# One tile of angles for all rotary tables, both halves of the Gram masks in one step, GpSimd's work given to VectorE, and new hand-over times in a two-layer decoder

## The chip, the cores and the metric

The kernel runs on one core of one Trainium2 chip. The metric is device time of one execution in microseconds (us), lower being better: 1338.36 us before, the median of three runs.

## What is computed

Two decoder layers on 512 tokens of width 1024, in float32. Each layer projects the normalized input once, splits the columns over three mixers, joins their outputs in a projection back, and ends in a SwiGLU feed-forward. The reference, cut:

```python
def layer(x):
    hn = rms_norm(x, g1)
    p = hn @ W_in                                   # columns for three mixers
    yA = rwkv7_mixer(p[..., :RW_IN])                # 4 heads x 64, delta-rule state, group norm, gate
    yB = retention_mixer(p[..., RW_IN:RW_IN+RET_IN], positions)   # 4 heads x 64, rotary q and k, decays
    yC = latent_attention(p[..., RW_IN+RET_IN:], positions)       # 8 heads, 64 + 32 rotary
    x = x + concat(yA, yB, yC) @ W_out
    return x + swiglu(rms_norm(x, g2))
...
def rope(x, positions):
    d = x.shape[-1]
    inv = ROPE_BASE ** (-arange(0, d, 2) / d)
    ang = positions[..., None] * inv
    x1, x2 = x[..., : d // 2], x[..., d // 2:]
    return concat([x1 * cos(ang) - x2 * sin(ang), x2 * cos(ang) + x1 * sin(ang)])
```

## The kernel before

**Tiles.** Activations lie feature-major, in tiles of 128 features by 512 tokens. A float32 product is made of three products of rounded halves: every operand is split in a high part and a low part (high + low = value), and `gemm` issues for each block of 128 input features (a k-step) high x high, low x high and high x low, so three matmuls of 128x512, all at line L244 (`mm`). Weights come by SP's DMA into `wr` (512 KB); ScalarE casts the high part `wh` (L404), VectorE subtracts to get the low part `wl` (L405), or GpSimd does it for the weights whose numbers stand in `POOL_LO`. There are three buffers of each. PSUM has four buffers `pd` (projections, attention scores) and four buffers `pm` (everything else).

**Order.** The stages are Python generators that a `Driver` resumes. Its clock counts modelled TensorE time; `yield T[l]["name"]` says how much of it passes before the generator is resumed, and the entries `p_...` are priorities. TensorE's instructions keep the order in which they are issued so; on the other engines a scheduler sets the order from when things are issued. The table `EN` gives many element-wise operations (`E("e595")` and the like) to VectorE (`d`), GpSimd (`p`) or ScalarE (`a`). So a number in `T` moves instructions on every engine.

**Rotary tables** (`tables`, `angles`, L527 to L583). The positions times a column of frequencies, reduced to [-pi, pi] by eight operations of VectorE, then Abs and two Sin of ScalarE. Done once for retention (`invr`, then a sign by GpSimd at L571, two DMAs to `tab_d`), once for the keys of attention in another layout, and once for its queries (`invm`, two DMAs at L580). L1131/L1132 and L1260/L1261 read the tables back.

**RWKV** (`rwkv`). Low-rank products (operands `LR`) give decay and gates. Sums over heads normalize the key (L656 takes their maximum with 1e-24, then L657, L663). Per block b of 128 channels, ScalarE makes three exponentials (L707 to L709), and four products make the operands of the Gram matrices: e592 (L716), e593 (L717), e594 (L718) on VectorE and e595 (L720) on GpSimd, with a small `dsc` (L721). L726 and L308 make and split the bonus term. Then four Gram groups (two per block) of 16 matmuls 64x128 each fill two `pm` buffers; L744 and L745 mask their parts into `GL` and `GR`, 32 operations of 128x256 per layer. L747 sends `GL` to `ms_d` for the solve of 31 steps (L792, L793). `chain` runs the eight chunks of each block one after the other and copies each output back into the operand `ar` (L862); `group_norm` splits it (casts L870 on ScalarE, subtractions h4 L871 on VectorE), forms mean and variance on TensorE, and ends at L882 to L887.

**Rotary step** (L1140 to L1145). L1140 scales a projection, four DMAs of SP swap its halves, GpSimd multiplies with cosine (e968, L1143) and sine (e969, L1144), VectorE adds (L1145). Attention's queries go through L1265 to L1272 (e1090, e1096, e1097) and L1285 into the score operands; `head` makes scores (TensorE, 96 rows), the maximum (L974), exp on ScalarE (L976), the reciprocal (L978) and the scaling (L979).

**Feed-forward.** Four pairs of gate and up projections are made plainly (L1343 to L1346), the rest in Strassen-Winograd form on 2x2 blocks of 128x512 weights (sums at L433, split at L422 and L423) and of tokens. `token_sums` (L1008 to L1052) makes the eight token operands B11, -T1, B22, -T2, B21, T4, T3, each a high and a low tile of 128x1024 (L1015 to L1029), handing over by `sums1` to `sums7`; TensorE uses them in the order -T1, B11, B22, -T2, a down projection, B21, T4.

Of the kernel before, what the change touches and what calls it, by code (L numbers as in the profile page):

```python
# [41 lines left out]
NU, NR, NW = 29, 8, 3  # L42

AHEAD, FETCH = 3, 2
POOL_LO = (20, 35, 38, 115, 137, 139)


def shape_constants():
# [142 lines left out]
def tile_trunk(ctx: ExitStack, tc: tile.TileContext, a: dict, out: bass.AP, dbg=None):  # L191
# [334 lines left out]
    def tables():  # L526
# [44 lines left out]
        for i, u in enumerate((co, si)):  # L571
            sp.dma_start(tab_d[i], u)
# [906 lines left out]
```

## Time and profile before

| | |
|---|---|
| median of three runs | 1338.36 us (1336.69 to 1338.86) |
| profiled execution | 1338.68 us, span 1336.9 us |
| mean granted clock of TensorE | 0.977 |
| TensorE busy | 1282.5 us (96%) |
| weight loads busy | 1095.1 us (82%) |
| VectorE busy | 993.8 us (74%) |
| ScalarE busy | 690.1 us (52%) |
| GpSimd busy | 123.0 us (9%) |

The span is the time from the first to the last instruction; the profiled execution's own time is 1.8 us more. PE is TensorE, PEld its weight loads, DVE VectorE, ACT ScalarE, POOL GpSimd, SP the engine that issues most DMAs. In a row of the timeline stand the start, the duration, engine, line, operation, what is written and read, the shapes and a count; in brackets is the idle time of the engine just before, with what ended it. The granted clock is 1.00 at full speed.

### The profile page before, as it was taken

Reading aid. Unit: us, or ns where it says so; the run is one execution under the profiler, and the core shown is the slowest. Engines: PE = TensorE matmul, PEld = TensorE weight load, DVE = VectorE, ACT = ScalarE, POOL = GpSimd, SP = SyncE. Lnnn points to the kernel's source line nnn. Section 1 sums busy time; section 2 is a strip of 40 time slices with the busy share of each in tenths; the row PEclk is TensorE's granted clock in tenths of the full one; section 3 lists DMA queues with packets and bytes.
Section 4 is the critical chain, followed back from the end, with each engine's and each line's share of the span. In section 5 each row is a group of like instructions: output and inputs, shape, how many; then the busy total and the mean of one; then the engine's idle time right before and its main releaser. Section 6 shows DMA issues by size and latency. Waiting matters only on the chain. (4 is left out here: it accounts for less than half of the span.)

```text
span 1336.9 us, 20195 instructions
## 1 busy us (share of the span) xinstructions
PE 1282.5 (96%) x7774; PEld 1095.1 (82%) x7774; DVE 993.8 (74%) x1672; ACT 690.1 (52%) x1279; POOL 123.0 (9%) x102
## 2 busy tenths in 40 slices
PE   7989999899899999999999898989999999999996
PEld 5768787578799999999877777846888999999994
DVE  7796877747977777777658696586579877777774
ACT  7844446726444444455475345556355545444553
POOL 0151131201000000000004400121010000000000
PEclk9989999999899999999999899979999999999998
DMA  7434421223142333333522424121222333322231
GB/s 243 129 96 135 93 79 55 79 64 111 35 139 96 100 106 95 100 107 101 183 88 83 126 78 85 33 95 63 79 95 79 111 106 100 110 96 95 82 109 63
DMA packets 65593, 131.04 MB, mean 98 GB/s; under 512 B 29045, under 2 KB 31765, under 8 KB 65497
## 3 DMA queue, kind: packets, MB, share of 16 engines
q1 hardware_dynamic: 64120, 128.14, 31.0%
q8 instruction: 61, 1.00, 0.3%
q10 hardware_dynamic: 1232, 1.09, 0.2%
q0 software_dynamic: 144, 0.52, 0.1%
q14 instruction: 36, 0.29, 0.1%
HBM read 117.40 MB, written 9.18 MB: 95 GB/s over the span
## 5 line engine op out<-in xcount | busy, mean ns | idle before, releaser
L244 PE MATMUL pd<-u,wh 128*128 128x256 f32 (+1 forms) x3112 | 760.8, 337 | 9.8 <-ACT wh L404 6.3
L244 PEld LDWEIGHTS pd<-u,wh 128*128 128x128 f32 x3112 | 531.0, 192 | 74.4 <-issue 7.8
L244 PE MATMUL pd<-u,wl 128*128 128x256 f32 (+1 forms) x1556 | 519.0, 334 | 1.4 <-DVE wl L423 1.4
L244 PEld LDWEIGHTS pd<-u,wl 128*128 128x128 f32 x1556 | 298.7, 192 | 30.6 <-DVE wl L423 1.9
L244 PE MATMUL pm<-u,wh 128*128 128x512 f32 (+1 forms) x800 | 212.1, 352 | 0.1
L404 ACT CAST wh<-wr 128x1024 fp32r<-128x1024 f32 (+3 forms) x102 | 98.8, 974 | 165.2 <-PE pd L244 97.2
L244 PEld LDWEIGHTS pm<-u,wh 128*128 128x128 f32 x800 | 139.1, 190 | 18.5 <-DVE u L1025 0.3
L405 DVE TENSOR_TENSOR wl<-wr,wh 128x1024 fp32r<-128x1024 f32 (+3 forms) x96 | 113.4, 1184 | 43.3 <-ACT wh L404 43.2
L244 PE MATMUL pm<-u,wl 128*128 128x512 f32 (+1 forms) x400 | 140.4, 351 | 0.0
L422 ACT CAST wh<-r 128x512 fp32r<-128x512 f32 x144 | 87.4, 618 | 101.5 <-PE pm L244 52.5
L422 ACT CAST wh<-wr 128x512 fp32r<-128x512 f32 x108 | 67.0, 620 | 78.3 <-PE pm L244 55.6
L423 DVE TENSOR_TENSOR wl<-r,wh 128x512 fp32r<-128x512 f32 x144 | 97.6, 687 | 9.4 <-ACT wh L422 7.5
L423 DVE TENSOR_TENSOR wl<-wr,wh 128x512 fp32r<-128x512 f32 x108 | 74.2, 689 | 24.2 <-ACT wh L422 22.0
L244 PEld LDWEIGHTS pm<-u,wl 128*128 128x128 f32 x400 | 75.7, 189 | 10.2
L244 PE MATMUL pm<-u,u 32*32 32x32 f32 (+4 forms) x728 | 70.9, 287 | 12.0 <-DVE u L718 5.0
L1381 DVE TENSOR_TENSOR u<-u,pm 128x512 f32<-128x512 f32 x64 | 43.7, 684 | 46.4 <-PE pm L244 46.4
L244 PEld LDWEIGHTS pm<-u,u 32*32 32x32 f32 (+3 forms) x728 | 53.0, 163 | 29.3 <-issue 15.1
L404 ACT CAST wh<-gg 128x1024 fp32r<-128x1024 f32 x32 | 33.6, 1049 | 43.5 <-issue 29.4
L244 PE MATMUL pd<-u,u 96*128 96x512 f32 (+3 forms) x128 | 49.5, 498 | 5.1 <-ACT u L976 3.5
L433 DVE TENSOR_TENSOR r<-r,wr 128x512 f32<-128x512 f32 x72 | 49.5, 687 | 0.6
L405 DVE TENSOR_TENSOR wl<-gg,wh 128x1024 fp32r<-128x1024 f32 x32 | 39.1, 1222 | 8.2 <-ACT wh L404 8.2
L685 POOL TENSOR_TENSOR u<-u,u 128x512 f32<-128x512 f32 x2 | 2.6, 1298 | 374.2 <-DMA u<-vf_d 369.3
(273 smaller groups left out, 1637.8 us busy)
## 6 DMA issues: line engine op xcount, KB each, us to landing
wr<-in_wts_dram SPq DMA_DIRECT2D x142, 512.0 KB, 3.5
gg<-in_wts_dram SPq DMA_DIRECT2D x32, 512.0 KB, 3.5
wr<-in_wts_dram SPq DMA_DIRECT2D x22, 384.0 KB, 3.0
u<-in_xT_dram SPq DMA_DIRECT2D x7, 512.0 KB, 6.0
tb<-tab_d SPq DMA_DIRECT2D x8, 256.0 KB, 4.5
r<-r SPq DMA_DIRECT2D x32, 64.0 KB, 2.0
h_d<-u SPq DMA_DIRECT2D x4, 512.0 KB, 2.9
u<-h_d SPq DMA_DIRECT2D x4, 512.0 KB, 3.6
```

The lines of the kernel that those rows point to most:

```text
L244: tc.keep_in_program_order(nc.tensor.matmul(o, lhsT, rhs, start=start, stop=stop, skip_group_check=True))
L404: act.copy(hi[:, z], t[:, z])
L405: (pool if on in POOL_LO else dve).tensor_tensor(lo[:, z], t[:, z], hi[:, z].bitcast(F32), ALU.subtract)
L422: act.copy(hi[:, z], t)
L423: dve.tensor_tensor(lo[:, z], t, hi[:, z].bitcast(F32), ALU.subtract)
L433: E(key).tensor_tensor(o, x, y, ALU.add)
L685: E("e563").tensor_tensor(vf[:, b, :], vf[:, b, :], v_[:, b, :], ALU.subtract)
L1381: dve.tensor_tensor(hk(m), hk(m), ps, ALU.add)
```

## The change

One tile of angles serves retention and attention: its first 64 rows hold the frequencies of retention with the sign folded in, the others those of attention. One pass of VectorE and ScalarE and GpSimd's sign are gone; the tile goes to `tab_d` in eight DMAs of 64x512 instead of four of 128x512. The sigmoid stands before the tanh (one table load of ScalarE less). `GL` and `GR` become parts of one tile `GG`, so a mask of 128x512 does what two of 128x256 did: 16 per layer; `ms_d` is sent in four parts per layer, each right behind its masks. The chain's output goes to a tile of its own (`Y`, the solve's old `TQ`), so the group norm splits it in one cast and one subtraction of 128x512. In `EN`, e595, e826, e969, e1037, e1090 and e1097 go from GpSimd to VectorE, c498 (one cast of 128x1024 per layer) from ScalarE to VectorE, h3 and h4 from VectorE to GpSimd. `POOL_LO` has other weights, the first among them. Most entries of `T` for layer 0 and some for layer 1 are new. All line numbers below the constants fall by 1 to 4.

```diff
-POOL_LO = (20, 35, 38, 115, 137, 139)
+POOL_LO = (0, 21, 26, 32, 35, 106, 115, 137)
...
-    add("invr", inv_r[i % 32][:, None])
-    add("invm", inv_m[i % 16][:, None])
+    add("inv", np.where(i < 32, -inv_r[i % 32], np.where(i < 64, inv_r[i % 32], inv_m[i % 16]))[:, None])
...
-        co, si = yield from angles(c("invr"))
-        pool.tensor_scalar(si, si, c("sgr"), None, ALU.mult)
+        co, si = yield from angles(c("inv"))
         for i, u in enumerate((co, si)):
-            sp.dma_start(tab_d[i], u)
-        ready["ret"] = True
+            for j in range(2):
+                for k in range(2):
+                    sp.dma_start(tab_d[2 * j + i, 64 * k : 64 * k + 64], u[64 * j : 64 * j + 64])
+        ready["ret"] = ready["mla"] = True
         yield T[0]["angles5"]
         yield from angles(None, True)
         ready["kr"] = True
-        yield T[0]["angles6"]
-        co, si = yield from angles(c("invm"))
-        for i, u in enumerate((co, si)):
-            sp.dma_start(tab_d[2 + i], u)
...
-        GL = [ur([P, NCH, 2, 64]) for _ in range(2)]
-        GR = [ur([P, NCH, 2, 64]) for _ in range(2)]
+        GG = [[ur([P, 4, 4, 64]) for _ in range(2)] for _ in range(2)]
+        GL = lambda b, n: GG[b][n // 4][:, n % 4, 1:3, :]
+        GR = lambda b, n: GG[b][n // 4][:, n % 4, 0:4:3, :]
...
-                    dve.tensor_tensor(GL[b][:, c4, par, :], v3[par][:, :, par, :], gmv[:, 0:1, :].broadcast_to([P, 4, 64]), ALU.mult)
-                    dve.tensor_tensor(GR[b][:, c4, 1 - par, :], v3[par][:, :, 1 - par, :], gmv[:, 1:2, :].broadcast_to([P, 4, 64]), ALU.mult)
+                    o = GG[b][i][:, :, 1 - par : 4 - par : 2, :]
+                    m = gm4[:, par].unsqueeze(1).broadcast_to([P, 4, 2, 64])
+                    dve.tensor_tensor(o, pg[par].rearrange("p (j w t) -> p j w t", j=4, w=2), m, ALU.mult)
...
-                E("c736").copy(ar[H[par], WT[1 - par]], pY[H[par], WT[1 - par]])
+                E("c736").copy(Y[H[par], b, n * 64 : n * 64 + 64], pY[H[par], WT[1 - par]])
...
-            E("c742").copy(n3(y[0][H[par]]), z)
-            E("h4").tensor_tensor(n3(y[1][H[par]]), z, n3(y[0][H[par]].bitcast(F32)), ALU.subtract)
+        y = halves(z, "h4")
...
-'sums1': 0.57, 'sums2': 0.48, 'sums3': 0, 'sums4': 2.67, 'sums5': 0, 'sums6': 4.34, 'sums7': 1.11
+'sums1': 0.4, 'sums2': 2.74, 'sums3': 5.14, 'sums4': 4.41, 'sums5': 5.79, 'sums6': 6.14, 'sums7': 5.45
```

The last pair of lines is the end of the table `T` for layer 0. What the new tables do to the order is shown at three places of VectorE's queue.

The first is the entry to the feed-forward of layer 0. L1343/L1339 and L1345/L1341 are the plain gate and up products, L1025/L1021 and L1029 token sums, L433/L432 weight sums, L423/L422 the low parts of the first Strassen weight (before | after). Before:

```order
L1025 TENSOR_TENSOR u_3202<-u_3196,u_3201 128x1024
L299 TENSOR_TENSOR u_3211<-r_700_3205,u_3211 128x512
L1029 TENSOR_TENSOR u_3196<-u_3142,u_3196 128x1024
L1346 TENSOR_TENSOR r_715_3286<-r_715_3286,r_716_3287 128x512
L433 TENSOR_TENSOR r_721_3300<-wr_3298 128x512
L1025 TENSOR_TENSOR u_3244<-u_3196,u_3243 128x1024
L1025 TENSOR_TENSOR u_3262<-u_3147,u_3261 128x1024
L299 TENSOR_TENSOR u_3292<-r_715_3286,u_3292 128x512
L423 TENSOR_TENSOR wl_3303<-r_721_3300,wh_3302 128x512
L423 TENSOR_TENSOR wl_3303<-wr_3296,wh_3302 128x512
```

And after, where wl_3214 is the low part of the last plain weight before them:

```order
L404 TENSOR_TENSOR wl_3214<-wr_3211,wh_3213 128x1024
L1025 TENSOR_TENSOR u_3121<-u_3201,u_3121 128x1024
L1021 TENSOR_TENSOR u_3207<-u_3201,u_3206 128x1024
L1339 TENSOR_TENSOR r_705_3246<-pd_3170,rB_3075 128x512
L1018 SCALAR_TENSOR_TENSOR u_3240<-u_3121,u_3239 128x1024
L1341 TENSOR_TENSOR r_706_3247<-pd_3210,rB_3075 128x512
L432 TENSOR_TENSOR r_711_3260<-wr_3258 128x512
L1342 TENSOR_TENSOR r_705_3246<-r_705_3246,r_706_3247 128x512
L422 TENSOR_TENSOR wl_3263<-wr_3256,wh_3262 128x512
L422 TENSOR_TENSOR wl_3263<-r_711_3260,wh_3262 128x512
```

The token sums of T4 and T3 (the last two L1025 of before) now stand behind these rows, and those of B21 too.

The second is the Gram stage of layer 1, from the operands of the second block to the first mask. Before, with e595 on GpSimd:

```order
L716 TENSOR_TENSOR u_7166<-u_6848,r_1352_7134 64x8x64 x2
L717 TENSOR_TENSOR u_7167<-u_6826,r_1353_7135 128x8x64
L718 TENSOR_TENSOR u_7167<-u_6710,r_1353_7135 128x8x64
L308 TENSOR_TENSOR r_1361_7179<-r_1358_7175,r_1360_7178 128x512
L1145 TENSOR_TENSOR u_6979<-u_6979,r_1342_7086 128x512
L726 SCALAR_TENSOR_TENSOR r_1359_7176<-u_6935,PC,u_6710 128x512
L405 TENSOR_TENSOR wl_7201<-wr_7198,wh_7200 128x864
L308 TENSOR_TENSOR r_1363_7184<-r_1359_7176,r_1362_7183 128x512
L1140 TENSOR_TENSOR r_1364_7187<-pd_7096,rB_6675 128x512
L744 TENSOR_TENSOR u_7225<-pm_7229,C 128x4x64
```

After, with e595 at L716 and e969 at L1140:

```order
L712 TENSOR_TENSOR u_7145<-u_6827,r_1349_7113 64x8x64 x2
L713 TENSOR_TENSOR u_7146<-u_6805,r_1350_7114 128x8x64
L1140 TENSOR_TENSOR r_1339_7065<-r_1339_7065,tb_6955 128x512
L714 TENSOR_TENSOR u_7146<-u_6689,r_1350_7114 128x8x64
L1141 TENSOR_TENSOR u_6958<-u_6958,r_1339_7065 128x512
L716 TENSOR_TENSOR u_7145<-u_6914,r_1348_7112 64x8x64 x2
L722 SCALAR_TENSOR_TENSOR r_1355_7154<-u_6914,PC,u_6689 128x512
L404 TENSOR_TENSOR wl_7180<-wr_7177,wh_7179 128x864
L722 SCALAR_TENSOR_TENSOR r_1356_7155<-u_6914,PC,u_6689 128x512
L1136 TENSOR_TENSOR r_1361_7166<-pd_7075,rB_6654 128x512
L1136 TENSOR_TENSOR r_1375_7237<-pd_7176,rB_6654 128x512
L742 TENSOR_TENSOR u_7204<-pm_7208,C 128x8x64
```

Two subtractions of h3 (L308) have left, e595, e969 and a second scaling (L1136) have come in, and the masks are twice as wide.

The third is the entry to attention of layer 1: L1285/L1281 builds a score operand, L974/L970 is the maximum. Before:

```order
L974 TENSOR_REDUCE nmx_8546<-pd_8543 128x1
L342 SCALAR_TENSOR_TENSOR r_1610_8526<-r_1611_8527,r_1610_8526 128x512
L974 TENSOR_REDUCE nmx_8556<-pd_8553 128x1
L883 TENSOR_TENSOR r_1609_8524<-pm_8483,r_1610_8526 128x512
L974 TENSOR_REDUCE nmx_8566<-pd_8563 128x1
L1285 TENSOR_TENSOR u_8514<-pd_8517,fB_8149 64x512
L978 RECIPROCAL rs_8550<-ssum_8548 128x1
L1285 TENSOR_TENSOR u_8514<-pd_8517,fB_8149 64x512
```

After:

```order
L1281 TENSOR_TENSOR u_8462<-pd_8471,fB_8122 64x512
L879 TENSOR_TENSOR r_1604_8481<-pm_8434,r_1605_8483 128x512
L1281 TENSOR_TENSOR u_8497<-pd_8500,fB_8122 64x512 x2
L970 TENSOR_REDUCE nmx_8517<-pd_8514 128x1
L970 TENSOR_REDUCE nmx_8527<-pd_8524 128x1
L970 TENSOR_REDUCE nmx_8537<-pd_8534 128x1
L970 TENSOR_REDUCE nmx_8547<-pd_8544 128x1
```

The maxima now follow the last score operand in one block. On TensorE two k-steps more stand ahead of the first score, taken from ahead of the group norm's sums, and in layer 0 the low-rank products stand in one block four k-steps later.

More of the change, by code (lines that the diff above doesn't have):

```diff
@@ new lines @@
+EN = {'e499': 'd', 'e535': 'd', 'e541': 'd', 'e542': 'p', 'e563': 'p', 'e564': 'p', 'e565': 'd', 'e592': 'd', 'e593': 'd', 'e594': 'd', 'e595': 'd', 'e757': 'p', 'e759': 'd', 'e773': 'p', 'e826': 'd', 'e968': 'p', 'e969': 'd', 'e970': 'd', 'e909': 'd', 'e1037': 'd', 'e1090': 'd', 'e1096': 'p', 'e1097': 'd', 'e1171': 'd', 'e302': 'd', 'e273': 'd', 'c511': 'a', 'c639': 'a', 'c646': 'a', 'c647': 'a', 'c686': 'a', 'c716': 'a', 'c736': 'a', 'c1008': 'a', 'c498': 'd', 'h1': 'd', 'h2': 'd', 'h3': 'p', 'h4': 'p', 'h5': 'd', 'h6': 'd', 's1': 'd', 's2': 'd', 's3': 'd', 's4': 'd', 'z': 'd'}
@@ L61, in shape_constants @@
     t = np.arange(64)
-    add("gm", np.concatenate([(j[:, None] < t[None, :]), (j[:, None] <= t[None, :])], 1))
+    left, right = j[:, None] < t[None, :], j[:, None] <= t[None, :]
+    add("gm4", np.concatenate([left, right, right, left], 1))
     same = i[:, None] // 64 == i[None, :] // 64
@@ L77, in shape_constants @@
     inv_m = np.float32(10000.0) ** (-np.arange(0, 32, 2, dtype=np.float32) / np.float32(32))
-    add("invr", inv_r[i % 32][:, None])
-    add("invm", inv_m[i % 16][:, None])
+    add("inv", np.where(i < 32, -inv_r[i % 32], np.where(i < 64, inv_r[i % 32], inv_m[i % 16]))[:, None])
     add("invk", np.broadcast_to(np.tile(inv_m, 4), (P, 64)))
-    add("sgr", np.where(i % 64 < 32, -1.0, 1.0)[:, None])
     return np.concatenate(cols, 1).astype(np.float32), where, exact
@@ L602, in rwkv @@
         z = st["xs1"]
+        act.activation(z[64:128], z[64:128], AF.Sigmoid)
         act.activation(z[0:32], z[0:32], AF.Tanh)
[L604 removed]
         zh, zl = halves(z, "h1")
@@ L832, in chain @@
     def chain(l, st, b):
-        AR, BKT, UV, GL, GR, X, dsc = st["chunk"]
+        AR, BKT, UV, GL, GR, X, dsc, Y = st["chunk"]
+        Y = Y.rearrange("p (b n) t -> p b (n t)", b=2)
         Sb = [sm((P, P), tag=f"Sb{b}", bufs=2) for _ in range(2)]
@@ L857, in chain @@
                 mm(pS, BKT[b][:, n, :], uv, False, True)
-            mm(pY, uv, GR[b][:, n, :, :], False, True)
+            mm(pY, uv, GR(b, n), False, True)
             if n < NCH - 1:
@@ L866, in group_norm @@
     def group_norm(l, st, b):
-        y, n3 = (r2(dt=F32R), r2(dt=F32R)), lambda t: t.rearrange("p (n t) -> p n t", t=64)
-        for par in range(2):
-            z = st["chunk"][0][b][H[par], :, WT[1 - par]]
-            E("c742").copy(n3(y[0][H[par]]), z)
-            E("h4").tensor_tensor(n3(y[1][H[par]]), z, n3(y[0][H[par]].bitcast(F32)), ALU.subtract)
+        z = st["chunk"][-1].rearrange("p (b n) t -> p b (n t)", b=2)[:, b, :]
+        y = halves(z, "h4")
         yield T[l]["group_norm1"]
```

20 lines of the change are left out of this document (8 added, 12 removed).

## The prediction

> **What bounds the kernel now.** I read the busy times first. TensorE is busy nearly all the time:
>
> ```profile
> PE 1282.5 (96%) x7774; PEld 1095.1 (82%) x7774; DVE 993.8 (74%) x1672; ACT 690.1 (52%) x1279; POOL 123.0 (9%) x102
> ```
>
> The execution profiled took 1338.68 us (span 1336.9; the median of the runs is 1338.36, so what I take off the one comes off the other). The change removes no matmul, so it can gain only where TensorE stands still or runs at a reduced clock. The waits of TensorE say where it stands still (columns: sum, times, longest):
>
> ```profile
> PE pd L244 <- ACT wh L404: 6.3, 1, 6.3
> PE pm L244 <- DVE u L718: 5.0, 1, 5.0
> PE pm L244 <- DVE u L745: 4.3, 2, 3.8
> PE pd L244 <- ACT u L976: 3.5, 1, 3.5
> ...
> PE pd L244 <- ACT wh L422: 2.3, 1, 2.3
> ...
> PE pd L244 <- DVE u L1285: 1.7, 1, 1.7
> ...
> PE pd L244 <- DVE wl L423: 1.4, 1, 1.4
> ```
>
> The first is the load at the start and stays. The other six, 18.2 us together, lie in four places: the Gram stage of layer 0, that of layer 1 (masks), the entry to the feed-forward of layer 0 (L422, L423), and the entry to attention in layer 1 (L976, L1285). The windows show a second loss there (after PE's busy time come PEld, DVE, ACT and POOL, then the granted clock):
>
> ```profile
> core 0: us, PE busy (x) PEld busy (x) DVE busy (x) ACT busy (x) POOL busy (x), PEclk, DMA share, GB/s
> 400.00:650.00 250.00, 250.00 (x1707) 233.17 (x1707) 191.46 (x288) 120.26 (x225) 0.00 (x0) 1.00 0.33 105
> ...
> 357.00:364.00 7.00, 5.35 (x23) 5.06 (x24) 6.58 (x10) 2.79 (x6) 0.00 (x0) 0.52 0.01 2
> 743.00:750.00 7.00, 5.41 (x35) 4.75 (x35) 5.05 (x14) 0.00 (x0) 5.75 (x7) 0.51 0.54 150
> 883.00:900.00 17.00, 14.31 (x39) 8.55 (x40) 12.69 (x37) 8.87 (x28) 5.57 (x5) 0.50 0.10 36
> ```
>
> In the feed-forward TensorE has no gap and its full clock: nothing is to be had there. After a stall it runs at half clock, for 7 us or for 17.
>
> **Entry to the feed-forward, layer 0.**
>
> ```profile
> 343.23 1.22 DVE L405 TENSOR_TENSOR wl<-wr,wh 128x1024 fp32r<-128x1024 f32 x1
> 344.37 1.22 DVE L1029 TENSOR_TENSOR u<-u,u 128x1024 f32<-128x1024 f32 x1
> ...
> 355.17 0.69 DVE L433 TENSOR_TENSOR r<-wr 128x512 f32<-128x512 f32 x1
> ...
> 358.65 0.69 DVE L423 TENSOR_TENSOR wl<-r,wh 128x512 fp32r<-128x512 f32 x1
> 359.25 0.69 DVE L423 TENSOR_TENSOR wl<-wr,wh 128x512 fp32r<-128x512 f32 x1
> ...
> 357.25 0.74 PE L244 MATMUL pd<-u,wh 128*128 128x256 f32 x2 [2.32 <-ACT wh L422]
> 359.39 0.58 PE L244 MATMUL pd<-u,wl 128*128 128x256 f32 x1 [1.40 <-DVE wl L423]
> ...
> 360.41 0.63 PE L244 MATMUL pd<-u,wh 128*128 128x256 f32 x2
> ...
> 361.05 0.63 PE L244 MATMUL pd<-u,wh 128*128 128x256 f32 x2
> ...
> 364.58 0.40 PE L244 MATMUL pd<-u,wh 128*128 128x256 f32 x2
> ...
> 364.94 0.40 PE L244 MATMUL pd<-u,wh 128*128 128x256 f32 x2
> ```
>
> VectorE works through nearly all token sums before it forms the first weight sum (L433). The new sums2 to sums7 spread them. In the new order seven operations lie between the last plain wl (343.23) and the two wl of the first part: three of 128x1024 (1.14 from start to start, 343.23 to 344.37) and four of 128x512 (0.60, 358.65 to 359.25); one more of 0.60 stands ahead of that plain wl. So the second wl ends at 343.23 + 0.60 + 1.14 + 3 x 1.14 + 4 x 0.60 + 0.60 + 0.69 = 352.1, not 359.94. TensorE arrives at 357.25 - 2.32 = 354.93: 2.8 us of slack, and both stalls (3.72) go. With them goes the half clock: a k-step takes 0.64 (360.41 to 361.05) where it takes 0.36 at 364.58; eight k-steps make 8 x 0.28 = 2.2. Next late is the down weight's wl, whose place in the queue comes near 361.0 when TensorE wants it at 361.05; I give back 0.4. **Term: -5.5** (ends -5.9 and -2, where a later part of the token sums stalls TensorE once).
>
> **Gram stage, layer 1.** TensorE's order is the same in both.
>
> ```profile
> 728.76 3.45 POOL L720 TENSOR_TENSOR u<-u,r 64x512 f32<-64x512 f32 x2
> ...
> 728.30 2.76 DVE L716 TENSOR_TENSOR u<-u,r 64x512 f32<-64x512 f32 x2 [0.87 <-ACT r L707]
> 731.09 1.67 DVE L717 TENSOR_TENSOR u<-u,r 128x512 f32<-128x512 f32 x1
> 732.68 0.68 DVE L718 TENSOR_TENSOR u<-u,r 128x512 f32<-128x512 f32 x1
> ...
> 743.71 0.41 DVE L744 TENSOR_TENSOR u<-pm,C 128x256 f32<-128x256 f32 x1
> 744.04 0.41 DVE L745 TENSOR_TENSOR u<-pm,C 128x256 f32<-128x256 f32 x1
> ...
> 744.59 2.70 PE L244 MATMUL pm<-u,u 64*128 64x128 f32 x16 [3.81 <-DVE u L745]
> ```
>
> While GpSimd runs e595 (L720), an operation of VectorE takes 1.67 where one of the same size takes 0.68: each costs the other about a microsecond. The Trainium skill ("SBUF — State Buffer", section "SBUF: two separate sides") says why: the two engines take one port pair by an exclusive lock for a whole instruction. The trace agrees in size (1.67 against 0.68). By that rule the first weight, h3 and h4, now GpSimd's, would block VectorE in turn, up to a microsecond for each of the nine operations if all meet one, against 16 operations of e595 and e969 that leave GpSimd.
>
> On VectorE e595 costs two of 64x512 for each block of 128 channels. I take 1.3 a pair (twice 0.6 and a tail), the row nearest to it without GpSimd beside it being L871's 1.40 below; the far end is L716's 3.44. From 728.30: both pairs of e592, e593, e594 and e595 (four pairs at 1.3, four at 0.6), the two of the rotary step that now stand there (1.2), h3's first two (1.4), one wl of 128x864 (about 1.0) and two L1140 (1.2): about 12.4 us in all, so the masks start near 740.7, not 743.71. A mask of double width costs 0.6 for two of 0.33, so the masks themselves gain nothing; but the third Gram's first matmul needs one mask (done at 741.3) where it needed two (done at 744.45). It starts some 3 us earlier; the stall falls from 3.81 to about 0.7, its last matmuls wait till 742.0, and the half clock (7 us at 0.51, worth 2 to 3) mostly goes. **Term: -4.5** (ends -5.5 and -1.5, the half clock staying and the swapped copy of L1140 coming late).
>
> **Gram stage, layer 0.**
>
> ```profile
> 70.69 3.44 DVE L716 TENSOR_TENSOR u<-u,r 64x512 f32<-64x512 f32 x2
> ...
> 84.98 0.41 DVE L744 TENSOR_TENSOR u<-pm,C 128x256 f32<-128x256 f32 x1
> ...
> 76.66 2.17 PE L244 MATMUL pm<-u,u 64*128 64x128 f32 x16 [5.03 <-DVE u L718]
> ...
> 85.87 0.46 PE L244 MATMUL pm<-u,u 64*128 64x128 f32 x2 [0.47 <-DVE u L745]
> ```
>
> The angles' second pass (eight operations of VectorE ahead of this, four of ScalarE behind it) is gone, and e592 to e595 run without GpSimd beside them, so the operands are there near 71 to 72, when TensorE arrives (71.6): the wait of 5.03 goes. Next late are again the masks: they follow the second pair's operands and two wl, 7.9 us, then one or two masks: 79.7 to 80.4 for the third Gram, which now starts at 85.87. Against it, the sums for the key norm (L656 before) now stand two k-steps after the low-rank matmuls instead of twelve, and their operands pass ScalarE behind six other operations: a new stall of up to 2.7 us near 52, with a half-clock stretch perhaps. It comes ahead of the third Gram, which waits for VectorE anyhow, so it is mostly absorbed. **Term: -4** (ends -5.5 and +0.5). Eight table DMAs instead of four lie ahead of the low-rank weights on SP; their matmuls stand four k-steps later and cover it. Nothing.
>
> **Entry to attention, layer 1.**
>
> ```profile
> 863.34 1.40 DVE L871 TENSOR_TENSOR r<-u,r 64x512 fp32r<-64x512 f32 x2 [0.76 <-ACT r L870]
> ...
> 881.53 0.68 DVE L974 TENSOR_REDUCE nmx<-pd 128x1 f32<-128x512 f32 x1
> ...
> 884.01 0.80 PE L244 MATMUL pd<-u,u 96*128 96x128 f32 x2 [3.46 <-ACT u L976]
> ...
> 886.59 2.08 PE L244 MATMUL pd<-u,u 96*128 96x512 f32 x2 [1.68 <-DVE u L1285]
> ```
>
> h4 leaves VectorE (two pairs of 1.40), e1097's add and four e1090 join it, and all four pairs of L1285 now come before the first reduce, which stays near 881 to 882. The four reduces follow each other (1.9 us), so the second exp is done near 883.4, and the fifth score starts then instead of 886.59: -3.2. The half clock still comes and, as before, lasts until the transposes. **Term: -3** (ends -7 without half clock, 0).
>
> The rest (one table load a layer, group norm of layer 0 with h4 on GpSimd, the first weight on GpSimd) I take at 0, between -2 and +3: GpSimd's 1.3 us for 0.68 there is hidden by six or more k-steps. **Sum: -5.5 - 4.5 - 4 - 3 = -17: 1321.** Its own range is 1314 to 1328, since the terms will not all fall at one end.
>
> **The rivals.**
> (1) *Given back*: the Gram stages come earlier, but the solve and the token sums, fed by the same VectorE, hold TensorE later. Half of the sum stays: -8.5, 1330. For it: VectorE is busy 74% of the span and takes on GpSimd's work. Against: layer 1 enters its feed-forward with its sums spread, and the waits on L422 and L423 stand there once each, both in layer 0.
> (2) *Deeper*: no stall trips the clock in attention (17 us at 0.50 cost up to 8): 1314.
> (3) *No clock to regain*. If the clock drops only after a long stall, the short ones at 357 and 359 cost none, and the sum loses 2.2 there and about 1.5 in the Gram stage: 1325. The row of 357.00:364.00 (0.52 behind stalls of 2.32 and 1.40) speaks against it. The Trainium skill ("TensorE: Matmul & The Clock Gate", Part 1) puts the drop after an idle window of about 3.4 us.
> (4) *It does nothing*: what is late is the masks, of the same total width, and each wait returns one step on: 1337.
> (5) *Slower*: the 1.4 to 1.7 us that VectorE needs for one of 64x512 in L716 is the price of that shape and not of GpSimd beside it. Then e595 on VectorE costs 3.44 a pair, both Gram stages have four such pairs in a row, and the masks start at 92.7 and 749.7: 7.7 and 6 us later, with a further half-clock stretch (1.7) each: +17, less 5.5 and 3, gives 1347. It decides at about 2.9 us a pair. Against it: L871's pair of the same shape, with both inputs in SBUF and GpSimd idle, takes 1.40.
>
> **How the numbers follow.** Forecast 0.59, (1) 0.15, (2) 0.10, (3) 0.03, (4) 0.06, (5) 0.07. A measurement tells 0.2%, 2.7 us, from no change. Faster: 0.59 + 0.15 + 0.10 + 0.03 = 0.87; same 0.06; slower 0.07. The range 1312 to 1333 takes in the forecast, (1) with its spread, (3) and most of (2); it leaves out (4), (5) and the rest of (2), less than 0.2.
>
> **What would show it.** Right: no wait on L422/L423 of before near 340 to 360 and a clock of 1.00 there; L716's pair near 1.3; third Gram 4 to 5 us earlier in each layer. Wrong: a pair of 64x512 still over 2.5 us on VectorE; new waits of TensorE on token sums or on the solve that add up to what the four places gain.

## The result and the profile after

The changed kernel takes 1317.26 us (median of four runs, 1314.65 to 1318.88) beside 1338.17 us for the one before (four runs, 1336.69 to 1338.86): a ratio of 0.9843, with a 95% interval of 0.9825 to 0.9862. That is 21 us less; the forecast was 17 less (1321), in a range of 1312 to 1333. The execution profiled below is the slowest of the four: 1318.88 us, span 1317.1 us, mean granted clock 0.983 (0.977 before).

The busy times of the changed kernel first:

```profile
PE 1274.7 (97%) x7774; PEld 1092.8 (83%) x7774; DVE 987.9 (75%) x1665; ACT 679.0 (52%) x1267; POOL 93.0 (7%) x82
```

TensorE still issues 7774 matmuls, and the span is 19.8 us shorter. Adding up the time between one matmul's end and the next one's start gives 41.6 us before and 30.2 now. Adding up the stretches of half clock (without the last one, at the very end) gives 51.2 us before and 37.6 now; an estimate from these: at half clock half of such a stretch is lost, so some 7 us of the gain are clock. Its waits, in the same columns as before (sum, times, longest):

```profile
PE pd L243 <- ACT wh L403: 5.9, 1, 5.9
PE pm L243 <- DVE u L742: 4.0, 2, 2.4
PE pm L243 <- ACT u L813: 3.2, 3, 2.1
PE pd L243 <- DVE u L1281: 2.9, 2, 1.6
...
PE pd L243 <- ACT u L972: 1.0, 1, 1.0
...
PE pd L243 <- DVE wl L422: 0.5, 1, 0.5
```

The wait of 5.0 for the Gram operands is gone, the 2.3 and 1.4 at the feed-forward entry have become one of 0.5 (L422), and attention's 3.5 and 1.7 are now 1.0 and 2.9 in smaller pieces. The masks' 4.3 (L742 is now what L744 and L745 were) are still 4.0. Each layer has 16 masks of 128x256 before and eight of 128x512 now; 32 and 16 are the numbers of both layers together.

Since both kernels issue the same number of matmuls, the start of the n-th matmul can be laid beside the start of the n-th. This table is made so; a negative number means that the changed kernel is ahead. Where the order differs the comparison holds only behind the place where both have done the same work:

```
place (us in the trace of before)        after - before   what that place gave
  58   low-rank products, layer 0              +3.6       +3.6   (1.1 of it before 20 us)
  95   behind layer 0's Gram groups            -2.5       -6.0   (the two together -2.5, by 320 -4.6)
 340   before the feed-forward of layer 0      -4.6
 400   in it                                  -10.4       -5.8
 700   before layer 1's mixing                -10.8       -0.4
 770   behind layer 1's Gram groups           -12.2       -1.4
 860   behind the solve and the chain         -14.7       -2.6
 890   in attention, layer 1                  -17.9       -3.2
1300   last stage                             -19.2       -1.3
```

**Entry to the feed-forward, layer 0.** The timeline of the changed kernel, VectorE's two low weights of the first part and then TensorE's k-steps:

```profile
345.36 0.70 DVE L422 TENSOR_TENSOR wl<-wr,wh 128x512 fp32r<-128x512 f32 x1
345.96 0.70 DVE L422 TENSOR_TENSOR wl<-r,wh 128x512 fp32r<-128x512 f32 x1
...
350.56 0.40 PE L243 MATMUL pd<-u,wh 128*128 128x256 f32 x2
...
350.92 0.40 PE L243 MATMUL pd<-u,wh 128*128 128x256 f32 x2
```

The two low weights of the first part are done at 346.66, before TensorE comes to their place near 350.3 (354.93 before, less the 4.6 that it is ahead), and a k-step takes 0.36 from start to start instead of 0.64. By the clock of before the second is done at 351.2; the forecast was 352.1.

**Gram stage, layer 0.** VectorE's pairs of 64x512 for e592 (L712) and e595 (L716), then the first mask and the third group:

```profile
68.86 1.38 DVE L712 TENSOR_TENSOR u<-u,r 64x512 f32<-64x512 f32 x2
...
71.47 1.40 DVE L716 TENSOR_TENSOR u<-u,r 64x512 f32<-64x512 f32 x2
...
74.41 1.16 PE L243 MATMUL pm<-u,u 64*128 64x128 f32 x16
...
81.97 1.27 DVE L742 TENSOR_TENSOR u<-pm,C 128x512 f32<-128x512 f32 x2
...
82.79 1.73 PE L243 MATMUL pm<-u,u 64*128 64x128 f32 x16 [1.59 <-DVE u L742]
```

A pair takes 1.38 us, as forecast (1.3), where it took 3.44. The first Gram group has no wait; the third waits 1.59 for a mask and starts 3.1 us earlier than before (forecast: 4 to 5).

**Gram stage, layer 1.** The same place in layer 1, with GpSimd's part of the bonus split (h3, L307):

```profile
717.49 1.69 DVE L712 TENSOR_TENSOR u<-u,r 64x512 f32<-64x512 f32 x2 [0.93 <-ACT r L703]
...
728.65 1.28 POOL L307 TENSOR_TENSOR r<-r,r 128x512 fp32r<-128x512 f32 x1 [6.78 <-issue]
728.70 1.78 DVE L722 SCALAR_TENSOR_TENSOR r<-u,PC,u 128x512 f32<-128x512 f32 x1
...
731.60 2.47 DVE L742 TENSOR_TENSOR u<-pm,C 128x512 f32<-128x512 f32 x4
732.42 2.64 PE L243 MATMUL pm<-u,u 64*128 64x128 f32 x16 [2.44 <-DVE u L742]
```

The third group starts 12.2 us earlier, of which TensorE was 10.8 ahead already, so 1.4 are of this place (forecast: 4 to 5). It waits 2.44, where about 0.7 was forecast, and its 16 matmuls take 2.64 (2.70 before): the half clock stays. The bonus product L722 takes 1.78 beside GpSimd and 0.75 without it (at 727.06).

**Entry to attention, layer 1.**

```profile
865.14 0.67 PE L243 MATMUL pd<-u,u 96*128 96x256 f32 x2 [1.60 <-DVE u L1281]
...
867.16 0.46 PE L243 MATMUL pd<-u,u 96*128 96x128 f32 x2 [1.29 <-DVE u L1281]
...
868.71 2.08 PE L243 MATMUL pd<-u,u 96*128 96x512 f32 x2 [1.03 <-ACT u L972]
```

Waits of 3.46 and 1.68 have become 1.60, 1.29 and 1.03, and the half clock behind them lasts 13.65 us instead of 17.07. The windows show what is left of reduced clock (after the five busy times the granted clock):

```profile
core 0: us, PE busy (x) PEld busy (x) DVE busy (x) ACT busy (x) POOL busy (x), PEclk, DMA share, GB/s
...
349.00:357.00 8.00, 8.00 (x60) 7.54 (x59) 7.87 (x13) 6.46 (x12) 0.00 (x0) 1.00 0.01 2
731.00:739.00 8.00, 6.58 (x40) 5.75 (x40) 6.83 (x12) 0.74 (x2) 7.58 (x9) 0.57 0.49 136
868.00:885.00 17.00, 16.29 (x55) 10.08 (x56) 12.33 (x41) 9.26 (x31) 3.73 (x3) 0.60 0.18 63
```

### The profile page after: what moved, and what is told of

Its sections match the earlier page's. It is cut to its first block, busy times and chain, and to the rows that moved or that the text cites. A ratio compares the mean times of both kernels' runs of the same rounds, so it can differ in the third digit from the quotient of the medians.

```text
span 1317.1 us, 20150 instructions
## 1 busy us (share of the span) xinstructions
PE 1274.7 (97%) x7774; PEld 1092.8 (83%) x7774; DVE 987.9 (75%) x1665; ACT 679.0 (52%) x1267; POOL 93.0 (7%) x82
## 5 line engine op out<-in xcount | busy, mean ns | idle before, releaser
L243 PEld LDWEIGHTS pd<-u,wh 128*128 128x128 f32 x3112 | 528.3, 191 | 71.6 <-issue 7.4
L403 ACT CAST wh<-wr 128x1024 fp32r<-128x1024 f32 (+3 forms) x102 | 98.9, 974 | 167.8 <-PE pd L243 105.2
L404 DVE TENSOR_TENSOR wl<-wr,wh 128x1024 fp32r<-128x1024 f32 (+3 forms) x93 | 109.2, 1177 | 45.2 <-ACT wh L403 44.8
L422 DVE TENSOR_TENSOR wl<-r,wh 128x512 fp32r<-128x512 f32 x144 | 97.6, 687 | 8.7 <-ACT wh L421 6.5
L422 DVE TENSOR_TENSOR wl<-wr,wh 128x512 fp32r<-128x512 f32 x108 | 74.3, 689 | 24.4 <-ACT wh L421 22.3
L403 ACT CAST wh<-gg 128x1024 fp32r<-128x1024 f32 x32 | 33.6, 1049 | 42.0 <-issue 27.7
L404 POOL TENSOR_TENSOR wl<-wr,wh 128x1024 fp32r<-128x1024 f32 (+2 forms) x9 | 18.9, 2100 | 491.4 <-ACT wh L403 491.4
L432 DVE TENSOR_TENSOR r<-r,wr 128x512 f32<-128x512 f32 x72 | 49.5, 687 | 0.6
L404 DVE TENSOR_TENSOR wl<-gg,wh 128x1024 fp32r<-128x1024 f32 x32 | 39.1, 1222 | 7.9 <-ACT wh L403 7.8
```

Source lines behind the costliest of these rows:

```text
L243: tc.keep_in_program_order(nc.tensor.matmul(o, lhsT, rhs, start=start, stop=stop, skip_group_check=True))
L403: act.copy(hi[:, z], t[:, z])
L404: (pool if on in POOL_LO else dve).tensor_tensor(lo[:, z], t[:, z], hi[:, z].bitcast(F32), ALU.subtract)
L422: dve.tensor_tensor(lo[:, z], t, hi[:, z].bitcast(F32), ALU.subtract)
L432: E(key).tensor_tensor(o, x, y, ALU.add)
```

## The experiments

The theory behind the forecast: four stalls of TensorE, each with a stretch of half clock, go because VectorE is freed of GpSimd's interference and because the new times bring its work in another order. Twelve kernels tried this. Ratios are to the kernel before, with 95% intervals; that kernel measured 1338.87, 1339.4 and 1339.81 us beside the three sets of four, 0.7 to 1.6 more than beside the changed kernel, so a difference between their times and 1317.26 can be too large by as much.

### The token sums' old times: e1_old_sums

The changed kernel with `sums1` to `sums7` of layer 0 as before:

```diff
-'sums1': 0.4, 'sums2': 2.74, 'sums3': 5.14, 'sums4': 4.41, 'sums5': 5.79, 'sums6': 6.14, 'sums7': 5.45
+'sums1': 0.57, 'sums2': 0.48, 'sums3': 0, 'sums4': 2.67, 'sums5': 0, 'sums6': 4.34, 'sums7': 1.11
```

> The changed kernel with the seven sums times of layer 0 of before; nothing else differs. Theory (the spread of the token sums frees VectorE for the first Strassen weight): the two stalls at the entry to the feed-forward of layer 0 come back at 2.3 and 1.4 us with 6.8 us of half clock, 5.5 to 6.5 us in all, so 1323 to 1324. Rival (VectorE has less to do ahead of it anyhow, with the group norm's work gone): the stalls come back at under 1 us, 1318 to 1319.

Measured: 1321.6 us (1318.99 to 1323.66), 0.9873 (0.9854 to 0.9891), 4.3 above the changed kernel. The two stalls are back in its timeline:

```profile
352.14 0.50 PE L243 MATMUL pd<-u,wh 128*128 128x256 f32 x2 [1.48 <-ACT wh L421]
...
354.28 0.58 PE L243 MATMUL pd<-u,wl 128*128 128x256 f32 x1 [1.64 <-DVE wl L422]
```

With them comes half clock (a k-step takes 0.64 from 355.30 on), and TensorE is 5.6 us behind the changed kernel in the feed-forward, 4.8 at the end. The term rests on these seven numbers, and e4_new_T and e3_old_T below agree: at this place the old code with new times gains 6.1 us, the new code with old times none.

### e595 back on GpSimd, and to VectorE alone: e2_e595_pool and e8_e595_dve

The changed kernel with one entry of `EN` back, and the kernel before with that entry alone changed:

```diff
-'e595': 'd'
+'e595': 'p'
```

> The changed kernel with e595 back on GpSimd; the scheduler may place other instructions anew. Theory (two engines on the same tiles hold each other up): VectorE's pair of 64x512 for e592 takes 2.4 to 3.4 us instead of 1.4, its 128x512 operations beside GpSimd 1.7 instead of 0.7; TensorE waits for Gram operands or masks 2 to 4 us longer in layer 0 and 1 to 2 us in layer 1, so 1320 to 1323. Rival (the long operations of before come of their shape): the pair stays at 1.4 and VectorE is 2.8 us per layer freer, so 1312 to 1316.

> The kernel before with e595 alone given to VectorE. Theory: VectorE's pair at e592 falls from 3.4 to 1.4 us, the Gram stall of layer 0 from 5.0 to 1 to 3 us, that of layer 1 from 3.8 to 2 to 3: 2 to 5 us less, 1333 to 1336. Rival (only together with the other moves): no change or slower, 1338 to 1341.

Measured: 1322.29 us (1320.03 to 1324.47), 0.9873 (0.9855 to 0.9891), for the first: 5 us lost, as expected. The second was missed: 1341.57 us (1339.88 to 1344.78), slower than before by a quarter of a per cent (1.0025, 1.0013 to 1.0036), where 3 to 6 us less were expected. Both traces agree on the price of meeting GpSimd. First e2's timeline, with e595 on GpSimd, then e8's, with it on VectorE:

```profile
67.99 3.90 POOL L716 TENSOR_TENSOR u<-u,r 64x512 f32<-64x512 f32 x2 [2.05 <-ACT r L704]
...
68.36 2.38 DVE L712 TENSOR_TENSOR u<-u,r 64x512 f32<-64x512 f32 x2
...
72.97 3.46 DVE L712 TENSOR_TENSOR u<-u,r 64x512 f32<-64x512 f32 x2
```

```profile
71.11 1.38 DVE L716 TENSOR_TENSOR u<-u,r 64x512 f32<-64x512 f32 x2
...
73.73 1.41 DVE L720 TENSOR_TENSOR u<-u,r 64x512 f32<-64x512 f32 x2
...
74.56 0.46 PE L244 MATMUL pm<-u,u 64*128 64x128 f32 x2 [2.51 <-DVE u L720]
...
85.03 0.46 PE L244 MATMUL pm<-u,u 64*128 64x128 f32 x2 [1.45 <-DVE u L745]
```

The pair of L716 falls from 3.44 to 1.38 by moving e595 alone. But VectorE then does e595 itself (1.41 and 1.38), which takes up most of what it saves: from the first pair to the first mask it needs 13.0 us, before 14.3. The first Gram wait halves (5.03 to 2.51), the masks come only 0.8 us earlier (third group at 85.03, before 85.87), and later TensorE waits 2.55 for a mask of retention beside layer 1's solve (806.12, for L932), with 10.24 us of half clock from 806.06 on. So the engine move does what was said to the operations, and by itself nothing for the time. In the changed kernel it is worth 5 us, and in the traces TensorE is 2.3 us ahead of e2's behind layer 0's Gram groups and 4.2 behind layer 1's. That VectorE has less to do ahead of the masks there is the likely reason, and no run tries it.

### Times and code apart: e3_old_T and e4_new_T

The changed code and engines with the whole table `T` of before, and the code of before with the new `T`.

> The changed kernel's code and engine table with the whole table of hand-over times of before. Theory (two of the four gains, feed-forward entry and attention entry, come of the times; the Gram gains come of the code and the engines): 1326 to 1330, with the Gram stages as in the changed kernel. Rival A (the times do nearly all): 1334 to 1338. Rival B (code and engines do nearly all): 1317 to 1322.

> The kernel before with the whole new table of hand-over times (the one entry it lacks kept as it was). Theory: the feed-forward entry loses its stalls (minus 6), the Gram stages keep theirs or lose more since GpSimd still runs e595 beside VectorE, and the times are set for work that is not there: 1328 to 1333. Rival A (the times do nearly all): 1317 to 1321. Rival B: 1336 to 1340.

Measured: 1332.67 us (1330.98 to 1338.56), 0.9957 (0.9942 to 0.9972), for the changed code with old times, a miss by some 3 us (its profiled execution took 1337.6); 1331.66 us (1331.1 to 1332.41), 0.9949 (0.9934 to 0.9964), for the old code with new times, as expected. So the code alone is worth 6.2 us, the times alone 7.2, and both 21: some 7 us come only from the two together. In layer 0's Gram stage the expectation for e3 failed: TensorE gains 2.5 us there and not 6.0. In layer 1's it held: e3 gains 1.4 like the changed kernel, e4 nothing. The next experiment, planned for another question, shows where a part of the 7 us lies.

### One tile of angles alone: e10_one_tile

The kernel before with this part of the change only:

```diff
-        co, si = yield from angles(c("invr"))
-        pool.tensor_scalar(si, si, c("sgr"), None, ALU.mult)
+        co, si = yield from angles(c("inv"))
         for i, u in enumerate((co, si)):
-            sp.dma_start(tab_d[i], u)
-        ready["ret"] = True
+            for j in range(2):
+                for k in range(2):
+                    sp.dma_start(tab_d[2 * j + i, 64 * k : 64 * k + 64], u[64 * j : 64 * j + 64])
+        ready["ret"] = ready["mla"] = True
...
-        co, si = yield from angles(c("invm"))
...
```

> The kernel before, with one part of the change alone: one tile of angles for all rotary tables. Theory: it frees VectorE some 5 us ahead of layer 0's Gram products, but these are held by the operands' splits, which meet GpSimd's; so 0 to 3 us less than before: 1336 to 1339 us, with layer 0's first Gram wait still over 3 us. Rival: the rotary tables' VectorE work is itself what makes the operands late, and the wait of 5.03 us shrinks below 1.5 us: 1332 to 1335 us.

Measured: 1343.08 us (1341.19 to 1346.47), 1.0024 (1.0013 to 1.0034). Neither expected value: it is slower. SP's queue, GpSimd's sign and the low-rank matmuls show where it loses. Before:

```profile
33.36 0.38 SPq L572 DMA_DIRECT2D tab_d<-r  x1
...
33.89 1.57 POOL L570 TENSOR_SCALAR r<-r,C 128x512 f32<-128x512 f32 x1 [32.13 <-ACT r L565]
...
35.49 0.33 SPq L572 DMA_DIRECT2D tab_d<-r  x1
...
36.34 0.57 SPq L591 DMA_DIRECT2D r<-in_rw_w_dram  x1
```

With one tile:

```profile
33.29 5.06 SPq L571 DMA_DIRECT2D tab_d<-r  x8
...
39.03 0.56 SPq L585 DMA_DIRECT2D r<-in_rw_w_dram  x1
...
43.05 0.38 PE L242 MATMUL pm<-LR,r 32*128 32x256 f32 x1 [0.51 <-ACT LR L296]
...
44.09 0.38 PE L242 MATMUL pm<-LR,r 32*128 32x256 f32 x1 [0.66 <-DVE r L306]
...
45.62 1.86 PE L242 MATMUL pm<-LR,r 32*128 32x256 f32 x7 [1.15 <-DVE LR L297]
```

Eight issues take SP 5.06 us. Before, it was 2.46 from the first issue to the end of the second, 0.7 for the two and 1.75 of waiting for GpSimd's sign (L570). So the low-rank weights behind them are asked for 2.7 us later (39.03, before 36.34). TensorE reaches their matmuls at 42.5, as before, and now waits 2.3 us there in three pieces, with 6.83 us of half clock from 44.98 on: it is 5.4 us behind at that place, and 5.3 at the end (by the medians 3.3). The casts and subtractions that it waits for stand behind those of a large weight there (L402 at 41.13, L403 at 42.21), where before they came first; that this order follows from the late issues is likely and not shown. The same three waits (0.38, 0.66, 1.15) stand in e3_old_T at 44.06 to 46.64, with the same half clock. The new times put these matmuls four k-steps later; in the changed kernel they start at 46.33 without a wait although SP's eight issues take 4.96 us there too. So the code brings a delay that the times hide, at the price of the half clock at 49.10. In the traces, behind layer 0's Gram groups (at 95 us), e3_old_T is 4.3 us behind the kernel before, e4_new_T 0.8 behind and the changed kernel 2.5 ahead: of the 12.0 us that by these traces only the two give together (e3's is of an execution of 1337.6), 7.5 are there by then. How these divide between the low-rank weights and the Gram operands wasn't separated. VectorE's freed time did not show: the first Gram wait is 3.46 (5.03 before) only because TensorE comes 5.4 us later.

### The low-rank matmuls set apart: e5_lr_apart

In the changed kernel the low-rank block ends in ten matmuls of 32 and 64 rows in a row, and a half clock begins in it (49.10, 6.83 us) though TensorE has no gap there. Here k-steps of a projection stand between them, as before the change:

```diff
-'rwkv4': 0, 'rwkv5': 0.0
+'rwkv4': 1.59, 'rwkv5': 1.05
```

> The changed kernel with two hand-over times of layer 0 as before (rwkv4 1.59, rwkv5 1.05), which sets the low-rank matmuls of 32 and 64 rows apart by k-steps again. In the changed kernel they stand in one block, TensorE never idles there, and yet it runs at half clock for 6.83 us right behind. Theory (matmuls on few rows count as little work for the clock): the half clock near 49 us is gone, TensorE reaches the first Gram up to 3 us earlier, but the third Gram is held by VectorE's masks, so at most 0 to 2 us of it remain: 1315 to 1318. Rival (the half clock there came of the waits at 8 to 17 us, or of chance): it stays at 5 us or more, same time.

Measured: 1333.19 us (1331.98 to 1334.33), 0.9951 (0.9939 to 0.9963): 16 us lost, a clear miss. The half clock at 49 is gone, and TensorE is 2.9 us earlier at that place, so that much was right (what decides it is told in the last section). But the key norm's maximum moves with it:

```profile
63.77 1.33 DVE L652 TENSOR_SCALAR r<-pm 128x512 f32<-128x512 f32 x2
```

It stands at 56.20 in the changed kernel. The Gram operands behind it are late, with a wait of 4.0 (for L716). Further waits follow, 5.7 at 163 (for L332) and 4.3 at 263 (for L975); that they come of the key norm too wasn't followed up. The forecast's worry, that the early key norm costs a stall of up to 2.7 us near 52, was the smaller side of that trade.

### What holds the third Gram group: e6_h3_dve, e7_masks_split, e9_late_bonus

Three edits of the changed kernel: h3 back on VectorE; every mask as two of 128x256; and the bonus step (L722 and the split behind it) issued between the second and the third Gram group instead of ahead of the first.

```diff
-'h3': 'p'
+'h3': 'd'
```

```diff
-                    dve.tensor_tensor(o, pg[par].rearrange("p (j w t) -> p j w t", j=4, w=2), m, ALU.mult)
+                    v = pg[par].rearrange("p (j w t) -> p j w t", j=4, w=2)
+                    for s in range(2):
+                        dve.tensor_tensor(o[:, :, s, :], v[:, :, s, :], m[:, :, s, :], ALU.mult)
```

```diff
-        ts = [r2(), r2()]
-        for b in range(2):
-            dve.scalar_tensor_tensor(ts[b], r_[:, b, :], col("rw_r_k", l, b), k_[:, b, :], ALU.mult, ALU.mult)
-            ts[b] = halves(ts[b], "h3")
...
+                if b == 0 and i == 1:
+                    ts = [r2(), r2()]
+                    for b_ in range(2):
+                        dve.scalar_tensor_tensor(ts[b_], r_[:, b_, :], col("rw_r_k", l, b_), k_[:, b_, :], ALU.mult, ALU.mult)
+                        ts[b_] = halves(ts[b_], "h3")
```

> The changed kernel with h3's two subtractions of each layer on VectorE instead of GpSimd. In the changed kernel VectorE's L722 beside GpSimd's L307 takes 1.78 instead of 0.75 in both layers, just ahead of the masks. Theory (GpSimd costs VectorE a microsecond there, and the two subtractions cost VectorE 1.2): the masks come 0 to 1.3 us later or earlier, the time is the same within 1 us, 1316 to 1319. Rival (h3 on GpSimd is a gain of its own): 1319 to 1321.

> The changed kernel with each mask of 128x512 made again by two operations of 128x256, into the same tile with the same constants. Theory (the width counts, not the number): each pair takes 0.66 to 0.75 us instead of 0.62, 1 to 2 us more VectorE in each layer, of which at most one pair lies ahead of the third Gram: 0 to +1 us, 1317 to 1318.5. Rival (half the masks is what brings the Grams forward): third Gram 1 us or more later in both layers with its half clock, 1319 to 1322.

> The changed kernel, with the step of the bonus sums (L722, and the split of its product on GpSimd) emitted between the second and the third group of Gram products instead of ahead of the first. Theory: the wait of 2.44 us ahead of layer 1's third Gram group and the 1.59 us ahead of layer 0's are the 1.78 us of L722, which stands ahead of the first mask on VectorE; with it behind, both waits go (under 0.5 us each) and layer 1's half clock at 731.76 (6.83 us) with them, so 3 to 6 us less than the changed kernel: 1311 to 1314 us. Rival: the wait only moves, to the bonus sums or to the masks that now stand behind L722, and the time is the changed kernel's, 1316 to 1319 us.

Measured: 1321.13 us (1317.99 to 1324.01), 0.9861 (0.9844 to 0.9878); 1318.9 (1317.13 to 1323.01), 0.9849 (0.9832 to 0.9867); 1318.24 (1317.64 to 1319.56), 0.9838 (0.9823 to 0.9853). All three intervals overlap the changed kernel's own. That the masks gain little by their shape is in line with e7, which lost at most 1.6 us by its median; in its trace layer 1's third group starts 0.88 us behind the first mask, in the changed kernel 0.82. For h3 the times settle nothing, but e6's trace of layer 1 speaks against blaming it:

```profile
730.48 1.90 DVE L722 SCALAR_TENSOR_TENSOR r<-u,PC,u 128x512 f32<-128x512 f32 x1
...
735.05 2.67 PE L243 MATMUL pm<-u,u 64*128 64x128 f32 x16 [3.89 <-DVE u L742]
```

With h3 on VectorE, L722 meets another operation of GpSimd (L404, 730.35 to 731.83) and takes 1.90, the first mask comes 15.6 us behind L712 instead of 14.1, and the third group waits 3.89 instead of 2.44. The third, e9, shows where the wait goes. Its timeline in layer 0 and layer 1:

```profile
80.09 1.16 PE L243 MATMUL pm<-u,u 64*128 64x128 f32 x16
...
90.05 0.65 PE L250 MATMUL pm<-ident,u 128*128 128x128 f32 x4 [1.62 <-DVE u L738]
```

```profile
729.64 1.75 PE L243 MATMUL pm<-u,u 64*128 64x128 f32 x16 [1.07 <-DVE u L738]
...
735.85 1.31 PE L243 MATMUL pm<-r,EX 128*128 128x512 f32 x4 [1.26 <-DVE u L738]
```

The third group starts 2.7 and 2.8 us earlier (80.09 for 82.79, 729.64 for 732.42; 1.1 and 1.4 of it TensorE was ahead before these stages), and layer 1's half clock there is gone. But the last masks now stand behind L722, and TensorE waits for them instead: 1.62 ahead of the solve's transposes, 1.26 ahead of the bonus sums. The 1.3 us that it gains on the changed kernel in layer 1's Gram stage are all given back by the end of the solve (half clock from 805.56 on, 3.41 us, which the changed kernel lacks). The rival holds: the wait moves. No version tried beats the changed kernel by what its runs can tell.

### Layer 1: e11_old_T1 and e12_attn_pool

The changed kernel with layer 1's row of `T` as before (20 entries, `p_att` 4.43 to 0 and `p_ret` 5.86 to 2.29 among them), and with three of attention's operations back on GpSimd:

```diff
-'e1037': 'd', 'e1090': 'd', 'e1097': 'd'
+'e1037': 'p', 'e1090': 'p', 'e1097': 'p'
```

> The changed kernel with layer 1's row of hand-over times as before (layer 0's row new). Theory: the new times of layer 1 give the gains at the solve and at the attention entry of layer 1 (2.6 and 3.2 us): 1320 to 1323 us, and the trace agrees with the changed kernel's up to about 700 us. Rival: these gains come from work taken off GpSimd, and the layer's times are worth nothing: 1316 to 1319 us.

> The changed kernel with the three attention instructions given to VectorE (e1037, e1090, e1097) back on GpSimd. Theory: the gain of 3.2 us at layer 1's attention entry comes from the hand-over times, and these three are worth under 1 us: 1316 to 1319 us. Rival: it comes from these three, and the wait at the entry grows back by about 3 us: 1320 to 1322 us.

Measured: 1318.93 us (1316.76 to 1322.28), 0.9849 (0.9827 to 0.9872), and 1318.8 us (1317.94 to 1321.25), 0.9844 (0.9828 to 0.986). Neither differs from the changed kernel by more than the runs spread. So the theory that layer 1's times give its gains falls: without them TensorE still gains 3.1 us at the attention entry (3.2 with them), though its one wait there is longer:

```profile
PE pd L243 <- DVE u L1281: 4.7, 1, 4.7
```

At the solve their trace is 1.3 us poorer, which the times of the runs can't tell. And the three operations are worth nothing that shows. What gives the 3.2 us is then in the rest of the code; e3_old_T, with that code and no new times at all, gains 2.2 us there. That it is h4, gone from VectorE, is an argument; no run tries it by itself.

## Why the prediction was right, step by step

**The feed-forward entry** (forecast -5.5; measured -5.8) held in every part: low weights before TensorE asks, both stalls gone, the k-step at 0.36, half a microsecond given back. Only the place of the last is another: the down weight is done at 356.16 when TensorE asks at 356.53, and the wait of 0.5 stands at a later weight sum (365.27). e1_old_sums takes the new times of the token sums away and loses 4.3 us.

**The Gram stage of layer 0** (forecast -4; measured -6.0 there, but +3.6 just ahead of it, and -4.6 when the layer's mixing is over) shows the forecast's mechanism: pairs at 1.38, the first wait gone, the masks next late (1.59). But the -6.0 is no measure of it, since a TensorE that comes late waits less: e4_new_T, with e595 still on GpSimd, comes 6.1 late and wins back 5.4. What the stage gave in all is -2.5, and another 2.1 came between 95 and 320 us, which no term had named. The count was short here as well: the first block's operands are done at 72.87 and not at 71 to 72, which costs no wait only because TensorE comes at 74.4 and not at 71.6. The first mask starts 9.1 us behind them and not 7.9, with an L722 of 1.77 beside L307 in between. Two things were not priced. The early low-rank block has its half clock from 49.10 on without any stall, where a stall was expected. And e8_e595_dve shows that the engine move is not enough: VectorE pays for e595 most of what it saves by no longer meeting GpSimd. The reason given for the gain (e592 to e595 "run without GpSimd beside them") is half of it; that the room that VectorE needs comes from the rest of the change is argued.

**The Gram stage of layer 1** (forecast -4.5; measured -1.4) is the term that was mis-sized. The step that failed is the count up to the masks, "about 12.4 us in all, so the masks start near 740.7", with the stall falling "to about 0.7" and the half clock that "mostly goes". Counted from the changed kernel's own L712, the first mask comes 14.1 us later (717.49 to 731.60). Of the 1.7 us too few, 1.0 is the two L722, which take 2.4 us instead of the 1.4 counted as "h3's first two", since the second has GpSimd's h3 beside it (1.78); the rest is the four pairs, 6.0 instead of 5.2, with a first one of 1.69. The prediction named that: h3 on GpSimd "would block VectorE in turn", and then did not count it. By e6_h3_dve the remedy is not to take h3 back, since L722 then meets another operation of GpSimd. Nor did it help that one mask is needed where two were: e7_masks_split, which needs two again, starts its third group 0.06 us later behind the first mask. With a wait of 2.44 the half clock stayed.

The first such meeting was told with a rule of the Trainium skill ("SBUF — State Buffer", section "SBUF: two separate sides"): one engine holds the shared port pair by an exclusive lock for a whole instruction, and the other blocks. The runs agree: moving e595 alone takes L716's pair from 3.44 to 1.38, and L722 takes 1.78 with L307 beside it and 0.75 without.

**The entry to attention** (forecast -3; measured -3.2) came out as counted: the first maximum starts at 867.04 and the fifth score at 868.71, by the clock of before (14.7 more) 881.7 and 883.4, where 881 to 882 and 883.4 were forecast. Which moved operation gives it is open: e1090 and e1097 are worth nothing by e12_attn_pool, and the half clock became one fifth shorter instead of staying as long.

**Taken at nothing**: the eight table DMAs, which "four k-steps later" cover. That was right (but for the number of before: two stand ahead of the low-rank weights there, not four), and e10_one_tile shows how much hung on it: in the old order the one tile costs 3.3 us by the medians. The rest, taken between -2 and +3, gave -4.3 in layer 1's solve and the last stages (-2.6, -1.3, and -0.4 ahead of them), and the 2.1 of layer 0 besides. The solve's part isn't settled: e7_masks_split and e9_late_bonus, with the same work there, have a half clock in it (from 807.64 and 805.56 on, 3.41 us each), and the changed kernel has none.

Together: -5.8 for -5.5, -2.5 for -4, -1.4 for -4.5, -3.2 for -3, and -6.4 (2.1 and 4.3) for 0 make -19.3, within 0.5 us of the span's -19.8. So the four terms gave 12.9 of the 17 forecast, and a third of the gain came where none was forecast. The entries to the feed-forward and to attention were right; that the sum was near is luck, since two terms too large and a rest too small cancelled.

**The rivals.** *Given back* was true of small things (e9_late_bonus is such a case) and not of the sum. *Deeper* has begun: attention's half clock is 3.4 us shorter. *No clock to regain* falls with the k-steps of e1_old_sums at 0.64 behind stalls of 1.48 and 1.64. The Trainium skill ("TensorE: Matmul & The Clock Gate", Part 1) puts the drop after an idle window of about 3.4 us. In e1_old_sums the longest gap there is 1.64, and the measurement decides. *It does nothing* describes the masks of layer 1 fairly and nothing else. *Slower*, by a pair of 64x512 that costs 3.44 by its shape, falls with the 1.38.

## What to carry to other kernels

Count what stands ahead of the first mask, not only what leaves the queue: an operation taken off GpSimd frees VectorE of a meeting and costs VectorE its own time. Here e595 on VectorE cost 0.25% alone (e8_e595_dve) and was worth 5 us beside the other moves (e2_e595_pool), so test a part both by adding it alone and by taking it away. For the one tile of angles only the first was done: alone it costs 3.3 us, and what it gives in the changed kernel is not known. When a wait of a microsecond or two goes, look for the half clock behind it, and for the next operand that is late.

## What the runs showed of the hardware

**Half clock without a gap.** Ten matmuls of 32 and 64 rows in a row, with TensorE never idle, are followed by half clock in the changed kernel. The same instructions, in the same order on every engine up to layer 1, ran without it in e11_old_T1. First the changed kernel, then e11:

```profile
48.02 3.92 PE L243 MATMUL pm<-r,LR 32*128 32x512 f32 x10
```

```profile
48.42 2.66 PE L243 MATMUL pm<-r,LR 32*128 32x512 f32 x10
...
54.75 0.50 PE L243 MATMUL pm<-r,EX 128*128 128x512 f32 x1 [1.61 <-ACT r L644]
```

In e11 the half clock comes later, behind the stall of 1.61 (56.01, 3.41 us), and by the end of the Gram stage TensorE is 1.5 us ahead of the changed kernel for no reason in the program. All stretches but the one at the very end last 3.41 us or a multiple of it (6.83, 10.24, 13.65, 17.07), and in each of the traces their starts lie whole multiples of 3.41 us apart. So each trace can be laid out in windows of 3.41 us, and this settles the low-rank block. In the changed kernel, e1, e2, e6, e7 and e9 its matmuls of 32 and 64 rows fill 2.7 us or more of one window, and half clock starts where that window ends. In e11 and e12 the block falls on two windows with 2.5 and 2.3 us at most, and none starts there; in before and in e5, with k-steps between, it is 1.9 at most, and none starts either. Both the few rows and the place of the block in the window count; where between 2.5 and 2.7 the limit lies these traces don't show. The Trainium skill ("TensorE: Matmul & The Clock Gate", Part 1) says that the clock is judged in windows of 3.4 us that run freely and don't start anew with the kernel. The lengths and starts in multiples of 3.41 us, at another place in each run, agree with that. It would account for runs of one kernel that differ by 4 us; that it does was not tried.

**Price of one DMA issue.** On SP the issue goes by the number of DMAs and not by their size. In the kernel before, a table DMA of 128x512 (256 KB) takes 0.38 and 0.33 us to issue, and a weight of 512 KB mostly 0.33 (L388, median of 174). In e10_one_tile each of the eight of 64x512 (128 KB) takes 0.45 to 0.70. A small load behind them, whose data TensorE needs at once, is late by what the larger number costs, less the 1.75 us that SP no longer waits for GpSimd.
